# A hybrid decoder layer on one core: the recurrence's copies scheduled ahead on VectorE, softplus summed inside the scan, and small VectorE steps given to ScalarE

## The chip, the cores and the metric

The kernel runs on one core of one Trainium2 chip. The metric is the device time of one execution in microseconds. Three executions of the kernel before took 1123.43, 1123.74 and 1125.81 us; their median, 1123.74 us, is what a change is held against. A further execution was taken by the hardware profiler, and all rows below come from it.

## The reference

One decoder layer on x of 512 tokens by 2048 channels, in float32. `h = rms(x)` is projected by `w_in`; the result is cut into three groups of heads, each computes its own mixing and is multiplied by a SiLU gate, and `w_out` projects all of it back onto the residual.

```python
def step(state, inp):                                   # A: 12 heads of 64, over 512 tokens
    r_t, k_t, v_t, w_t, kk_t, a_t = inp
    sa = einsum('bhvk,bhk->bhv', state, -kk_t)
    state = state * w_t + sa * (kk_t * a_t) + v_t * k_t
    return state, einsum('bhvk,bhk->bhv', state, r_t)
# before it: k = k * (1 + (a - 1) * k_a); after it: a norm per head, a bonus, the gate
d = trailing_mean(u, win) - u;  yb = (d @ pool_w) * pool_scale * silu(pg)          # B
z = rms(q) @ rms(k).T                                   # C: 12 heads, blocks of 128 queries
log_1m = where(causal, log_sigmoid(-z), 0)
after = reverse_cumsum(log_1m) - log_1m
w = where(causal, exp(log_sigmoid(z) + after), 0);  yc = (w @ v) * silu(gc)
x = x + concat([ya, yb, yc]) @ w_out
```

## The kernel before

**Projections.** Everything is laid out with channels on the 128 partitions and the 512 tokens along the free axis. The input projection has 57 column tiles (`tile_order`); three are done at the start from weights that are loaded early (`first`), 54 by `project`. To keep float32 accuracy with fast matmuls, each operand is split in a high and a low part: a weight half (128 x 1024, `raw`) is loaded by DMA, ScalarE casts it to `wh`, VectorE computes `wl = raw - wh`, and each k tile takes three matmuls of 512 columns (`three`: hh with wh, hl with wh, hh with wl). That makes 2592 projection matmuls into `pj` banks and 768 output matmuls into `oacc` banks. `wh` and `wl` have two buffers each. VectorE takes a finished tile out of its bank (`u = pj * rstd`).

**The side tasks.** For each of six pairs of RWKV heads there is a generator `rwkv(p)`, for each of six pairs of attention heads `attention(p)`, and four `pooling(g)`. After every projection matmul `pump()` resumes each task whose next moment has come. `rwkv(p)` first prepares decays and keys, then the mask products `gm`, then inverts 32 x 32 blocks by forward substitution on VectorE (`xblk`, `pr`; the data go through DRAM, `s`), then completes the inverse on TensorE (`q`). Its last part is the recurrence itself, over eight chunks of 64 tokens. Each chunk is a step of three links that depend on each other:

- W: `wus <- uv, amr` on TensorE; VectorE copies it in two halves to `wsb`; GpSimd makes `se`, the decayed state, meanwhile.
- U: `wus <- wsb, lt`; VectorE copies two halves into `uv`.
- S: `wus <- uv, bkt`; VectorE combines it with `se` into the next chunk's `uv`, two instructions. Two y products stand beside.

The page's names for the copies are `wsb<-wus`, `uv<-wus` (COPY, link U) and `uv<-wus,ec,se` (SCALAR_TENSOR_TENSOR, link S). The recurrence of pair p can only begin when that of pair p - 1 is over. `attention(p)` makes z for each head in three blocks (512, 512 and 256 wide), and for each block softplus, a mask, a scan backwards along the keys, a subtraction, a second mask and an exponential; `wT` are the transposed weights.

**What sets the order.** The code is traced in Python, and a scheduler then orders each engine's instructions by priority, which is the order of tracing unless `tc.high_priority(offset=n)` moves an instruction n places ahead. When a task is resumed is decided by the class `Pace`: it keeps a reckoned time `now`, which grows with every matmul, and for each other engine a list of booked stretches. `record` books an instruction in the first free stretch on its engine after its inputs are ready (`place`), and notes when its output will be ready. A task that waits for tiles gives back `need(..., margin)`, and goes on when `now` has passed their reckoned moment plus the margin: MARGIN = 2.5 us, TIGHT = 0.8 us inside the recurrence. The output projection begins when all pairs' tasks are done or forced through; `Y_ORDER` has pair 5 near its end. Scratch tiles come from a ring of TP = 16 buffers.

Of the kernel before, what the change touches and what calls it, by code (L numbers as in the profile page):

```python
# [13 lines left out]
P = 128  # L14
D = 2048
T = 512
# [37 lines left out]
MARGIN = 2.5  # L54
TIGHT = 0.8
AHEAD = 300
EVACUATE = 25
DL = 4.0
TP = 16

# [34 lines left out]
class Pace:  # L95
# [3 lines left out]
    def __init__(self):  # L99
        self.now = 0.0  # L100
        self.ready = {}
        self.read = {}
        self.busy = {"dve": [], "act": [], "pool": []}
        self.slots = {}
        self.queue = 0.0

    @staticmethod
# [103 lines left out]
def hybrid_trunk_kernel(ctx: ExitStack, tc: tile.TileContext, x, xT, w_in, w_out, vecs, consts, up_w, pool_w, out):  # L211
# [58 lines left out]
    bone_r = cp.tile([P, P], F32R, name="bone_r")  # L270
    bmean_r = cp.tile([P, P], F32R, name="bmean_r")
    biases = cp.tile([P, 4], F32, name="biases")
# [3 lines left out]
    nvec = cp.tile([P, 14], F32, name="nvec")  # L276

    def load_constants():
        dma(out=kon, in_=consts)
        dve.tensor_copy(out=bone_r, in_=bone)  # L280
        dve.tensor_scalar(bmean_r, bone, 1.0 / HD, None, ALU.mult)
        dve.tensor_scalar(nvec[:, 0:12], vec[:, V_W0:V_W0 + 12], -1.0, None, ALU.mult)
        dve.tensor_scalar(nvec[:, 12:13], vec[:, V_QN:V_QN + 1], HD ** -0.5, None, ALU.mult)

# [249 lines left out]
    def rwkv(p):  # L534
# [188 lines left out]
        for cc in range(NC_):  # L723
# [5 lines left out]
            wsb = rp.tile([P, C], F32, tag="wsb", bufs=2, name=name("wsb"))  # L729
            dve.tensor_copy(out=wsb[lo, :], in_=wps[lo, 0:C])  # L730
            dve.tensor_copy(out=wsb[hi, :], in_=wps[hi, C:P])
            if not last:
                se = rp.tile([P, C], F32, tag="se", bufs=2, name=name("se"))
                for h, s, o in quad:
                    pool.tensor_scalar(se[s, :], uv[s, cc, h, :], ec[s, cc:cc + 1], None, ALU.mult)
            yield need(wsb, lt, tag="y" if cc % 4 == 0 else None, margin=TIGHT)
# [4 lines left out]
            mm(yps, uv[:, cc, :, :], amr[:, cc, 2:4, :], True, False)  # L741
            dve.tensor_copy(out=uv[lo, cc, 0, :], in_=ups[lo, :])
            dve.tensor_copy(out=uv[hi, cc, 1, :], in_=ups[hi, :])
            yield need(uv, margin=TIGHT + 0.1)
            if not last:
                mm(sps, bkt[:, cc, :], uv[:, cc, :, :])
                for h, s, o in quad:
                    dve.scalar_tensor_tensor(uv[s, cc + 1, h, :], sps[s, h * C:(h + 1) * C], ec[s, cc:cc + 1], se[s, :], ALU.mult, ALU.add)
            mm(yps, uv[:, cc, :, :], rx[:, cc, :, :], False, True)
# [27 lines left out]
    def attention(p):  # L777
# [23 lines left out]
        for h in range(2):  # L801
# [5 lines left out]
            dve.tensor_tensor(q2[other, :], q[s, :], q2[s, :].bitcast(F32), ALU.subtract)  # L807
            dve.tensor_copy(out=k2[s, :], in_=kr[s, :])
            act.copy(out=k2[other, :], in_=k[s, :])
# [4 lines left out]
            for segs, width in ((((3, 0),), 512), (((2, 0), (0, 384)), 512), (((1, 0),), 256)):  # L814
                yield need(q2, k2, kl2, tag="g")
                z = gb("z")
                for i, off in segs:
                    mm(z[:, off:off + (i + 1) * P], q2[:, i * P:(i + 1) * P], k2[:, 0:(i + 1) * P], True, False)
                    mm(z[:, off:off + (i + 1) * P], q2[:, i * P:(i + 1) * P], kl2[:, 0:(i + 1) * P], False, True)
                zz = z[:, 0:width]  # L820
                n = ap.tile([P, 512], F32, tag="n", bufs=2, name=name("n"))
                n = n[:, 0:width]
# [8 lines left out]
                diag = lambda t: t[:, d0:d0 + nd * P].rearrange("p (a t) -> p a t", a=nd) if nd > 1 else t[:, d0:d0 + P]  # L831
                pool.affine_select(out=diag(n), in_=diag(n), pattern=pat, compare_op=ALU.is_gt, fill=0.0, base=0, channel_multiplier=1)
                w = ap.tile([P, width], F32, tag=f"w{segs[0][0]}{h}", name=name("w"))
                for i, off in segs:
# [3 lines left out]
                pool.affine_select(out=diag(w), in_=diag(w), pattern=pat, compare_op=ALU.is_gt, fill=-1e5, base=0, channel_multiplier=1)  # L838
                act.activation(w, w, AF.Exp)
# [16 lines left out]
        for js, width in (((0,), 512), ((1, 3), 512), ((2,), 256)):  # L856
            parts = []
            for h in range(2):
# [259 lines left out]
```

## Time and profile before

| | |
|---|---|
| median of three runs | 1123.74 us |
| the profiled execution | 1124.78 us |
| its span, first to last instruction | 1123.1 us |
| TensorE busy | 1023.5 us, 91% |
| VectorE busy | 733.7 us, 65% |
| ScalarE busy | 427.2 us, 38% |
| GpSimd busy | 228.0 us, 20% |
| mean granted TensorE clock | 0.941 |

Engines stand in the profile as PE (TensorE matmuls), PEld (its weight loads), DVE (VectorE), ACT (ScalarE), POOL (GpSimd) and SP (SyncE, which issues the DMAs). A busy share is an average over the whole span; the stages of this kernel differ, so a window's row tells more. Tile names are those of the program without buffer numbers. Nearly all instructions of VectorE, ScalarE and GpSimd carry one line, that of the helper that records them, so they are found by tile.

### The profile page before, as it was taken

The numbers are of one execution on the slowest core, as the hardware profiler recorded it, in microseconds if no ns is written. First come the engines' busy times: TensorE is split into PE (matmuls) and PEld (weight loads), VectorE is DVE, ScalarE is ACT, GpSimd is POOL, SyncE is SP. The second block draws the span as 40 slices with busy tenths as digits, with TensorE's granted clock in tenths as the row PEclk, the third lists the DMA queues.
The fourth block names the chain that finished last, engine by engine and source line by source line (L and its number), as shares of the span: only waits on it lengthen the run. The fifth ranks groups of instructions, "written<-read, shape, count | busy, mean of one in ns | idle before, by whom it ended". The sixth has DMA issues, their size and how long they took to land.

```text
span 1123.1 us, 13956 instructions
## 1 busy us (share of the span) xinstructions
PE 1023.5 (91%) x5084; PEld 818.0 (73%) x5084; DVE 733.7 (65%) x1554; ACT 427.2 (38%) x658; POOL 228.0 (20%) x330
## 2 busy tenths in 40 slices
PE   8989999899989999999999989999986067999998
PEld 7768777777877778877777777877764055888887
DVE  6278976788779768786797598955774433433232
ACT  6463534543455333652354355423431002312111
POOL 0131310442044112440133114213221010000000
PEclk9999999999999999998999999999995555999999
DMA  8522232131321232212323123232120111833232
GB/s 319 196 79 93 86 103 90 57 98 62 113 80 57 85 104 89 91 70 75 95 84 104 72 75 95 78 115 74 68 103 7 36 33 46 290 133 131 94 131 76
DMA packets 62229, 109.19 MB, mean 97 GB/s; under 512 B 29776, under 2 KB 31184, under 8 KB 62160
## 3 DMA queue, kind: packets, MB, share of 16 engines
q1 hardware_dynamic: 62160, 108.30, 28.7%
q8 instruction: 40, 0.66, 0.2%
q14 instruction: 29, 0.24, 0.1%
HBM read 98.84 MB, written 9.44 MB: 96 GB/s over the span
## 4 chain that ended last, share of the span: by engine, by line
PE 54%; DVE 21%; issue 9%; ACT 6%; POOL 5%; DMA 4%; SPq 0%; DVEq 0%; POOLq 0%; ACTq 0%
PE pj L367 26%; PE oacc L367 16%; DVE wl L205 4%; PE wus L367 4%; POOL e L205 3%; DVE w L205 3%; DVE xblk L205 2%; ACT e L205 2%; DVE pr L205 2%; DVE uv L205 2%; PE first L367 1%; ACT wh L205 1%; PE y L367 1%; DVE u L205 1%; PE o L367 1%
## 5 line engine op out<-in xcount | busy, mean ns | idle before, releaser
L367 PE MATMUL pj<-hh,wl 128*128 128x512 f32 x864 | 346.5, 401 | 6.8 <-DVE wl L205 6.8
L367 PE MATMUL pj<-hh,wh 128*128 128x512 f32 x864 | 346.4, 401 | 0.5 <-DVE u L205 0.4
L367 PE MATMUL pj<-hl,wh 128*128 128x512 f32 x864 | 346.7, 401 | 0.0
L205 DVE TENSOR_TENSOR wl<-raw,wh 128x1024 fp32r<-128x1024 f32 x140 | 175.8, 1256 | 137.6 <-ACT wh L205 137.1
L205 ACT CAST wh<-raw 128x1024 fp32r<-128x1024 f32 x140 | 146.7, 1048 | 296.5 <-PE pj L367 163.8
L367 PEld LDWEIGHTS pj<-hh,wl 128*128 128x128 f32 x864 | 164.2, 190 | 44.1 <-DVE wl L205 11.5
L367 PEld LDWEIGHTS pj<-hh,wh 128*128 128x128 f32 x864 | 164.2, 190 | 36.0 <-issue 4.7
L367 PEld LDWEIGHTS pj<-hl,wh 128*128 128x128 f32 x864 | 164.1, 190 | 34.9 <-issue 2.8
L367 PE MATMUL oacc<-wh,yh 128*128 128x512 f32 x256 | 101.2, 396 | 0.8 <-ACT yh L205 0.8
L367 PE MATMUL oacc<-wl,yh 128*128 128x512 f32 x256 | 101.0, 394 | 0.0
L367 PE MATMUL oacc<-wh,yl 128*128 128x512 f32 x256 | 100.5, 393 | 0.0
L205 POOL TENSOR_SCALAR se<-uv,ec 64x64 f32<-64x64 f32 x84 | 45.4, 541 | 220.8 <-DVE uv L205 202.8
L205 POOL TENSOR_SCALAR e<-e 128x512 f32<-128x512 f32 x28 | 45.4, 1622 | 123.5 <-ACT e L205 101.9
L367 PEld LDWEIGHTS oacc<-wh,yh 128*128 128x128 f32 x256 | 48.9, 191 | 11.6 <-ACT yh L205 1.0
L367 PEld LDWEIGHTS oacc<-wl,yh 128*128 128x128 f32 x256 | 48.8, 191 | 9.9
L367 PEld LDWEIGHTS oacc<-wh,yl 128*128 128x128 f32 x256 | 48.6, 190 | 10.0
L205 POOL TENSOR_TENSOR d<-u 128x512 f32<-128x512 f32 x25 | 36.5, 1461 | 79.0 <-DVE u L205 52.3
L205 DVE TENSOR_TENSOR pr<-xblk,nblk 128x60 f32<-128x60 f32 (+8 forms) x180 | 40.3, 224 | 16.2 <-DMA xblk<-s 9.7
L205 ACT ACTIVATE e<-e 128x512 f32<-128x512 f32 x50 | 31.5, 629 | 40.3 <-POOL e L205 39.8
L205 DVE TENSOR_TENSOR xblk<-xblk,pr 128x60 f32<-128x60 f32 (+8 forms) x180 | 41.4, 230 | 5.3
L205 DVE TENSOR_TENSOR_SCAN w<-kon,n 128x512 f32<-128x512 f32 (+3 forms) x48 | 38.8, 829 | 6.9 <-POOL n L205 6.9
L205 DVE TENSOR_TENSOR u<-pj,rstd 128x512 f32<-128x512 f32 x50 | 34.3, 685 | 11.8 <-PE pj L367 11.3
(204 smaller groups left out, 1353.3 us busy)
## 6 DMA issues: line engine op xcount, KB each, us to landing
raw<-in_w_in SPq DMA_DIRECT2D x108, 512.0 KB, 3.5
raw<-in_w_out SPq DMA_DIRECT2D x32, 512.0 KB, 4.3
lt<-in_x SPq DMA_DIRECT2D x8, 512.0 KB
xr<-in_x SPq DMA_DIRECT2D x16, 256.0 KB, 6.2
out<-xr SPq DMA_DIRECT2D x16, 256.0 KB, 3.6
yin<-yd SPq DMA_DIRECT2D x14, 256.0 KB, 4.0
fr<-in_w_in SPq DMA_DIRECT2D x12, 256.0 KB, 6.2
nblk<-s SPq DMA_DIRECT2D x24, 128.0 KB, 4.1
```

Of the source, the lines that this page charges most:

```text
L205: return call(*args, **kw)
L367: pe.matmul(o, lhsT, rhs, start=start, stop=stop)
```

## The change

`Pace` gets a mark `urgent`. While it is set, an instruction's reckoned end is its inputs' time plus 0.4 us plus its cost, with no booking of the engine. The new context `urgent()` sets it, and raises the priority of what is traced inside by SCAN = 150 places. The wsb copies with the se products, the uv copies, and the state combination of each step stand inside it. TIGHT falls from 0.8 to 0.5, and TP from 16 to 15.

In the attention a block of z is first copied to SBUF by ScalarE and masked there with -1e5; ScalarE makes log(1 + exp(-|w|)) and Relu(w) from the masked copy; the scan adds both operands as it goes, instead of a VectorE addition and a scan against ones; the second mask falls away. The scan over decays is one instruction for eight chunks: its multiplicand `fresh` is 1 except for a 0 at each chunk's first token. To ScalarE go Newton's square and affine step, the k_a step, the copies of transposed values, a cast of k, and one half of the wT copies.

```diff
-TIGHT = 0.8
+TIGHT = 0.5
+SCAN = 150
-TP = 16
+TP = 15
...
-        end = self.place(eng, at, self.cost(eng, f, out, ins))
+        if self.urgent:
+            end = at + 0.4 + self.cost(eng, f, out, ins)
+        else:
+            end = self.place(eng, at, self.cost(eng, f, out, ins))
...
+    @contextmanager
+    def urgent():
+        with tc.high_priority(offset=SCAN):
+            pace.urgent = True
+            yield
+            pace.urgent = False
...
-        dve.tensor_tensor(t, y0, y0, ALU.mult)
+        act.activation(t, y0, AF.Square)
         dve.scalar_tensor_tensor(t, ms, eps, t, ALU.add, ALU.mult)
-        dve.tensor_scalar(t, t, -0.5, 1.5, ALU.mult, ALU.add)
+        act.activation(t, t, AF.Copy, scale=-0.5, bias=1.5)
...
-        for j in range(NC_):
-            cj = slice(j * C, (j + 1) * C)
-            dve.tensor_tensor_scan(c[:, cj], unit.to_broadcast([P, C]), lam[:, cj], 0.0, ALU.mult, ALU.add)
+        dve.tensor_tensor_scan(c, fresh, lam, 0.0, ALU.mult, ALU.add)
...
-        dve.tensor_scalar(a, a, 1.0, col(V_KA), ALU.subtract, ALU.mult)
-        dve.scalar_tensor_tensor(kp, a, 1.0, ks, ALU.add, ALU.mult)
+        act.activation(a, a, AF.Identity, scale=col(V_KA), bias=nvec[:, 13 + p:14 + p])
+        dve.tensor_tensor(kp, a, ks, ALU.mult)
...
-                dve.tensor_copy(out=uv[dst, par::2, h, :], in_=vt4[src, :, h, :])
+                act.copy(out=uv[dst, par::2, h, :], in_=vt4[src, :, h, :])
...
-            dve.tensor_copy(out=wsb[lo, :], in_=wps[lo, 0:C])
-            dve.tensor_copy(out=wsb[hi, :], in_=wps[hi, C:P])
-            if not last:
-                se = rp.tile([P, C], F32, tag="se", bufs=2, name=name("se"))
+            with urgent():
+                dve.tensor_copy(out=wsb[lo, :], in_=wps[lo, 0:C])
+                dve.tensor_copy(out=wsb[hi, :], in_=wps[hi, C:P])
+                if not last:
+                    se = rp.tile([P, C], F32, tag="se", bufs=2, name=name("se"))
...
-                act.activation(n, zz, AF.Abs)
-                act.activation(n, n, AF.Exp, scale=-1.0)
-                act.activation(n, n, AF.Ln, bias=1.0)
-                dve.scalar_tensor_tensor(n, zz, 0.0, n, ALU.max, ALU.add)
...
+                act.copy(out=w, in_=z[:, 0:width])
+                pool.affine_select(out=diag(w), in_=diag(w), pattern=pat, compare_op=ALU.is_gt, fill=-1e5, base=0, channel_multiplier=1)
+                act.activation(n, w, AF.Abs)
+                act.activation(n, n, AF.Exp, scale=-1.0)
+                act.activation(n, n, AF.Ln, bias=1.0)
+                act.activation(m, w, AF.Relu)
...
-                    dve.tensor_tensor_scan(w[:, sg][:, ::-1], unit.to_broadcast([P, (i + 1) * P]), n[:, sg][:, ::-1], 0.0, ALU.mult, ALU.add)
-                dve.tensor_tensor(w, zz, w, ALU.subtract)
+                    dve.tensor_tensor_scan(n[:, sg][:, ::-1], n[:, sg][:, ::-1], m[:, sg][:, ::-1], 0.0, ALU.add, ALU.add)
+                dve.tensor_tensor(w, w, n, ALU.subtract)
...
-                (dve.tensor_copy if h == 0 else act.copy)(out=wt, in_=tps[:, 0:width])
+                act.copy(out=wt, in_=tps[:, 0:width])
```

TensorE's order in the first step of pair 5's recurrence. Before, it stands behind the last projection matmul, and its links follow each other directly (wus are the links, y the products beside them):

```order
L367 MATMUL wus_7782<-uv_7769,amr_95 128x128
L367 MATMUL y_7791<-amr_95,uv_7769 128x128
L367 MATMUL wus_7782<-wsb_7784,lt_97 128x64
L367 MATMUL wus_7782<-uv_7769,bkt_7755 128x128
L367 MATMUL y_7791<-rx_7295,uv_7769 128x128
L367 MATMUL wus_7799<-uv_7769,amr_95 128x128
```

With the change, the same step stands in the projection (pj), after 2414 of its 2592 matmuls:

```order
L377 MATMUL wus_7483<-uv_7427,amr_98 128x128
L377 MATMUL pj_7445<-hh_105,wl_7376 128x512
L377 MATMUL pj_7445<-hh_106,wh_7375 128x512
L377 MATMUL pj_7445<-hl_122,wh_7375 128x512
L377 MATMUL pj_7445<-hh_106,wl_7376 128x512
L377 MATMUL pj_7445<-hh_107,wh_7375 128x512
L377 MATMUL pj_7445<-hl_123,wh_7375 128x512
L377 MATMUL pj_7445<-hh_107,wl_7376 128x512
L377 MATMUL wus_7483<-wsb_7485,lt_100 128x64
L377 MATMUL y_7499<-amr_98,uv_7427 128x128
```

Seven projection matmuls stand between links W and U, where none did.

VectorE's order in the first step of the second recurrence, pair 1. Before, from the wsb copies to the uv copies of the U link (lt, amr and rx are pair 2's mask products):

```order
L205 COPY wsb_3408<-wus_3406 64x64 x2
L205 TENSOR_TENSOR lt_96<-gm_3422,kon 64x4x64
L205 TENSOR_TENSOR amr_94<-gm_3422,kon 64x4x64
L205 TENSOR_TENSOR rx_3304<-gm_3422,kon 128x4x64
L205 TENSOR_TENSOR lt_96<-gm_3423,kon 64x4x64
L205 TENSOR_TENSOR amr_94<-gm_3423,kon 64x4x64
L205 TENSOR_TENSOR rx_3304<-gm_3423,kon 128x4x64
L205 COPY uv_3291<-wus_3406 64x64 x2
```

With the change, the same step and the beginning of the next:

```order
L210 COPY wsb_2837<-wus_2835 64x64 x2
L210 TENSOR_TENSOR cq_2664<-u_2654,qs_2665 128x512
L210 TENSOR_TENSOR sl_2827<-qs_2824,sh_2826 128x512
L210 COPY uv_2746<-wus_2835 64x64 x2
L210 TENSOR_SCALAR sq_2753<-ss_2869 128x512
L210 TENSOR_TENSOR q_505_3079<-cq_2664,q_505_3079 64x512
L210 SCALAR_TENSOR_TENSOR uv_2746<-wus_2835,ec_1764,se_2840 64x64 x2
L210 SCALAR_TENSOR_TENSOR c_2875<-fresh,e_2846 128x512
L210 COPY wsb_2898<-wus_2896 64x64 x2
```

The copies of successive links now have one or two wide instructions between them (the row c<-fresh is the single scan).

## Rows read from the trace of the kernel before

**Rows 1.** The page: busy time by engine, and the granted clock in 40 slices.
```profile
PE 1023.5 (91%) x5084; PEld 818.0 (73%) x5084; DVE 733.7 (65%) x1554; ACT 427.2 (38%) x658; POOL 228.0 (20%) x330
...
PEclk9999999999999999998999999999995555999999
```

**Rows 2.** Windows: stretch, length, busy us of each engine (count), clock, DMA.
```profile
60.00:841.00 781.00, 745.09 (x3884) 595.07 (x3882) 603.09 (x1278) 344.53 (x543) 210.94 (x289) 0.98 0.26 86
...
841.40:949.00 107.60, 52.79 (x221) 37.39 (x222) 43.32 (x160) 9.77 (x19) 8.82 (x22) 0.51 0.08 20
...
112.00:140.00 28.00, 26.39 (x119) 21.30 (x118) 26.71 (x60) 15.94 (x29) 10.81 (x16) 1.00 0.26 87
...
833.00:843.00 10.00, 8.96 (x48) 6.41 (x47) 6.34 (x21) 1.35 (x3) 2.93 (x6) 1.00 0.00 1
...
949.00:1119.50 170.50, 170.34 (x745) 140.55 (x743) 55.72 (x61) 38.87 (x43) 0.00 (x0) 0.99 0.42 145
```

**Rows 3.** Timeline of TensorE, 829 to 900 us: start, length, instruction, [idle before <- what ended it].
```profile
829.63 0.80 PE L367 MATMUL oacc<-wh,yh 128*128 128x512 f32 x1 [0.82 <-ACT yh L205]
...
845.00 0.79 PE L367 MATMUL wus<-uv,amr 128*128 128x128 f32 x2 [0.27 <-DVE uv L205]
...
849.25 0.76 PE L367 MATMUL wus<-uv,amr 128*128 128x128 f32 x2 [0.36 <-DVE uv L205]
...
899.98 0.28 PE L367 MATMUL q<-xt,lt 32*32 32x32 f32 x2 [32.66 <-DVE xt L205]
```

**Rows 4.** Timeline of TensorE, 838 to 842 us, recurrence steps among output matmuls.
```profile
838.16 0.38 PE L367 MATMUL wus<-uv,amr 128*128 128x128 f32 x2
...
838.52 0.47 PE L367 MATMUL oacc<-wh,yl 128*128 128x512 f32 x1
838.83 0.40 PE L367 MATMUL oacc<-wh,yh 128*128 128x512 f32 x1
839.09 0.43 PE L367 MATMUL wus<-wsb,lt 128*128 128x64 f32 x2
839.34 0.48 PE L367 MATMUL oacc<-wl,yh 128*128 128x512 f32 x1
...
841.43 0.46 PE L367 MATMUL wus<-uv,amr 128*128 128x128 f32 x2 [0.56 <-DVE uv L205]
```

**Rows 5.** Who waited for tile wus, 60 to 841 us; timeline around 800 us.
```profile
  PE wus L367: 13.7, 10
...
799.82 0.75 DVE L205 SCALAR_TENSOR_TENSOR u<-po,vec,u 128x512 f32<-128x512 f32 x1 [2.34 <-POOL u L205]
...
801.00 0.43 PE L367 MATMUL wus<-wsb,lt 128*128 128x64 f32 x2 [2.27 <-DVE wsb L205]
```

**Rows 6.** VectorE's groups by form: count, busy us, mean ns, idle before.
```profile
L205 DVE TENSOR_TENSOR wl<-raw,wh 128x1024 fp32r<-128x1024 f32 x140 | 175.8, 1256 | 137.6 <-ACT wh L205 137.1
...
L205 DVE SCALAR_TENSOR_TENSOR n<-z,n 128x512 f32<-128x512 f32 x24 | 16.1, 680 | 6.9 <-ACT n L205 6.8
L205 DVE TENSOR_TENSOR_SCAN w<-kon,n 128x512 f32<-128x512 f32 x12 | 14.8, 1237 | 4.5 <-POOL n L205 4.5
...
L205 DVE TENSOR_TENSOR_SCAN c<-kon,e 128x64 f32<-128x64 f32 x48 | 10.5, 280 | 14.8 <-ACT e L205 14.7
...
L205 DVE COPY uv<-vt 64x256 f32<-64x256 f32 x24 | 10.1, 422 | 3.4 <-PE vt L371 3.0
...
L205 DVE TENSOR_TENSOR qs<-y 128x512 f32<-128x512 f32 x12 | 9.3, 772 | 3.5 <-ACT y L205 3.4
```

**Rows 7.** ScalarE's groups by form.
```profile
L205 ACT ACTIVATE n<-n 128x512 f32<-128x512 f32 x48 | 29.0, 627 | 0.5
...
L205 ACT COPY yc<-y 64x256 f32<-64x256 f32 x24 | 8.7, 364 | 61.8 <-PE y L367 61.6
```

**Rows 8.** Timeline of GpSimd around 500 us and 916 us: pairs of se.
```profile
500.18 2.64 POOL L205 TENSOR_SCALAR se<-uv,ec 64x64 f32<-64x64 f32 x2
...
916.33 0.97 POOL L205 TENSOR_SCALAR se<-uv,ec 64x64 f32<-64x64 f32 x2 [3.26 <-DVE uv L205]
```

More of the change, by code (lines that the diff above doesn't have):

```diff
@@ L1 @@
 import math
-from contextlib import ExitStack
+from contextlib import ExitStack, contextmanager
 import concourse.bass as bass
@@ L105, in __init__ @@
         self.queue = 0.0
+        self.urgent = False
     @staticmethod
@@ L271, in hybrid_trunk_kernel @@
     bmean_r = cp.tile([P, P], F32R, name="bmean_r")
+    fresh = cp.tile([P, T], F32, name="fresh")
+    pool.memset(fresh, 1.0)
+    pool.memset(fresh[:, 0:T:C], 0.0)
     biases = cp.tile([P, 4], F32, name="biases")
@@ L275, in hybrid_trunk_kernel @@
     eps_rms, eps_gn, neg_half = biases[:, 0:1], biases[:, 1:2], biases[:, 2:3]
-    nvec = cp.tile([P, 14], F32, name="nvec")
+    nvec = cp.tile([P, 20], F32, name="nvec")
     def load_constants():
@@ L282, in load_constants @@
         dve.tensor_scalar(nvec[:, 0:12], vec[:, V_W0:V_W0 + 12], -1.0, None, ALU.mult)
+        dve.tensor_scalar(nvec[:, 13:19], vec[:, V_KA:V_KA + 6], -1.0, 1.0, ALU.mult, ALU.add)
         dve.tensor_scalar(nvec[:, 12:13], vec[:, V_QN:V_QN + 1], HD ** -0.5, None, ALU.mult)
@@ L729, in rwkv @@
             wsb = rp.tile([P, C], F32, tag="wsb", bufs=2, name=name("wsb"))
-            dve.tensor_copy(out=wsb[lo, :], in_=wps[lo, 0:C])
-            dve.tensor_copy(out=wsb[hi, :], in_=wps[hi, C:P])
-            if not last:
-                se = rp.tile([P, C], F32, tag="se", bufs=2, name=name("se"))
-                for h, s, o in quad:
-                    pool.tensor_scalar(se[s, :], uv[s, cc, h, :], ec[s, cc:cc + 1], None, ALU.mult)
+            with urgent():
[3 more added lines that the diff above has]
+                    se = rp.tile([P, C], F32, tag="se", bufs=2, name=name("se"))
+                    for h, s, o in quad:
+                        pool.tensor_scalar(se[s, :], uv[s, cc, h, :], ec[s, cc:cc + 1], None, ALU.mult)
             yield need(wsb, lt, tag="y" if cc % 4 == 0 else None, margin=TIGHT)
@@ L741, in rwkv @@
             mm(yps, uv[:, cc, :, :], amr[:, cc, 2:4, :], True, False)
-            dve.tensor_copy(out=uv[lo, cc, 0, :], in_=ups[lo, :])
-            dve.tensor_copy(out=uv[hi, cc, 1, :], in_=ups[hi, :])
+            with urgent():
+                dve.tensor_copy(out=uv[lo, cc, 0, :], in_=ups[lo, :])
+                dve.tensor_copy(out=uv[hi, cc, 1, :], in_=ups[hi, :])
             yield need(uv, margin=TIGHT + 0.1)
@@ L746, in rwkv @@
                 mm(sps, bkt[:, cc, :], uv[:, cc, :, :])
-                for h, s, o in quad:
-                    dve.scalar_tensor_tensor(uv[s, cc + 1, h, :], sps[s, h * C:(h + 1) * C], ec[s, cc:cc + 1], se[s, :], ALU.mult, ALU.add)
+                with urgent():
+                    for h, s, o in quad:
+                        dve.scalar_tensor_tensor(uv[s, cc + 1, h, :], sps[s, h * C:(h + 1) * C], ec[s, cc:cc + 1], se[s, :], ALU.mult, ALU.add)
             mm(yps, uv[:, cc, :, :], rx[:, cc, :, :], False, True)
@@ L807, in attention @@
             dve.tensor_tensor(q2[other, :], q[s, :], q2[s, :].bitcast(F32), ALU.subtract)
-            dve.tensor_copy(out=k2[s, :], in_=kr[s, :])
+            act.copy(out=k2[s, :], in_=k[s, :])
             act.copy(out=k2[other, :], in_=k[s, :])
@@ L819, in attention @@
                     mm(z[:, off:off + (i + 1) * P], q2[:, i * P:(i + 1) * P], kl2[:, 0:(i + 1) * P], False, True)
-                zz = z[:, 0:width]
-                n = ap.tile([P, 512], F32, tag="n", bufs=2, name=name("n"))
-                n = n[:, 0:width]
-                act.activation(n, zz, AF.Abs)
-                act.activation(n, n, AF.Exp, scale=-1.0)
-                act.activation(n, n, AF.Ln, bias=1.0)
-                dve.scalar_tensor_tensor(n, zz, 0.0, n, ALU.max, ALU.add)
                 d0 = segs[0][0] * P
@@ L831, in attention @@
                 diag = lambda t: t[:, d0:d0 + nd * P].rearrange("p (a t) -> p a t", a=nd) if nd > 1 else t[:, d0:d0 + P]
-                pool.affine_select(out=diag(n), in_=diag(n), pattern=pat, compare_op=ALU.is_gt, fill=0.0, base=0, channel_multiplier=1)
                 w = ap.tile([P, width], F32, tag=f"w{segs[0][0]}{h}", name=name("w"))
+                act.copy(out=w, in_=z[:, 0:width])
+                pool.affine_select(out=diag(w), in_=diag(w), pattern=pat, compare_op=ALU.is_gt, fill=-1e5, base=0, channel_multiplier=1)
+                n = ap.tile([P, 512], F32, tag="n", bufs=2, name=name("n"))[:, 0:width]
+                m = ap.tile([P, 512], F32, tag="m", bufs=1, name=name("m"))[:, 0:width]
+                act.activation(n, w, AF.Abs)
+                act.activation(n, n, AF.Exp, scale=-1.0)
+                act.activation(n, n, AF.Ln, bias=1.0)
+                act.activation(m, w, AF.Relu)
                 for i, off in segs:
                     sg = slice(off, off + (i + 1) * P)
-                    dve.tensor_tensor_scan(w[:, sg][:, ::-1], unit.to_broadcast([P, (i + 1) * P]), n[:, sg][:, ::-1], 0.0, ALU.mult, ALU.add)
-                dve.tensor_tensor(w, zz, w, ALU.subtract)
-                pool.affine_select(out=diag(w), in_=diag(w), pattern=pat, compare_op=ALU.is_gt, fill=-1e5, base=0, channel_multiplier=1)
+                    dve.tensor_tensor_scan(n[:, sg][:, ::-1], n[:, sg][:, ::-1], m[:, sg][:, ::-1], 0.0, ALU.add, ALU.add)
+                dve.tensor_tensor(w, w, n, ALU.subtract)
                 act.activation(w, w, AF.Exp)
```

## The prediction

> **What bounds the kernel now.** I read the page's totals first. TensorE is busy 1023.5 of 1123.1 us, and the row of granted clock shows a full clock almost everywhere except for a hole near the end [rows 1]. The table of windows sizes that hole [rows 2]. From 60 to 841 us TensorE is busy 745.1 of 781 us at clock 0.98; from 841.4 to 949 us it is busy only 52.8 of 107.6 us, at 0.51; from 949 us on it is busy without a gap (745 matmuls in 170.3 us, so 0.2286 us each). The reader is to see three stages: a nearly full one, a hole of 107.6 us, a full one.
>
> The timeline of TensorE says what the hole is [rows 3]. With the last projection matmuls done, the recurrence of pair 4 still has four steps to go, and the whole of pair 5's follows: half of its mask products, 32.66 us of waiting for the block inverse that runs through VectorE and DMA, then eight steps. A step alone, at half clock, takes 4.25 us from one W matmul to the next (845.00 to 849.25), and TensorE waits within it for VectorE's copies. So the bound here is a dependent chain with nothing left to put between. The output projection doesn't fill it: two of its first four accumulators take g banks, which the recurrence still uses, and TensorE's order has them behind it.
>
> Why are the recurrences so late? In the first stage a step's matmuls don't stand close together: the order spreads the eight steps of one recurrence over 409 to 518 projection matmuls. The pace reckons each copy behind all the work booked on VectorE, and emits the next link only when that reckoning lets it. The chain itself is faster: where only a few output matmuls stood between, at full clock, W to W took 3.27 us (838.16 to 841.43) [rows 4].
>
> **The change, the reckoning.** With the copies marked urgent and TIGHT at 0.5, the order has each recurrence inside 129 to 164 wide matmuls (6 or 7 between two links), and the sixth is over at projection matmul 2558 of 2592, before the output projection begins. The hole's cause is gone: **minus 107.6 us**. Its matmuls have to be issued all the same, between others and at full clock: 52.8 us busy at a granted 0.51 is **plus 26.9 us** at full clock. A check from the other side [rows 4]: W with its y product takes 0.36 us to the next wide matmul (838.16 to 838.52), S with its own about as much, U 0.25, and each return to a wide matmul costs 0.08 (0.47 against 0.40), some 1.2 us a step; the 12 steps of the hole are 14.5 us, and the mask products, norms, transposes and block products an estimated 8 more. I take 26.9 and keep 22 as its lower bound.
>
> **What the copies cost now.** Behind a link stand only 6 or 7 matmuls of 0.2286 us, so with its own matmuls about 1.8 us from link to link, where the chain alone needs about 1.1 (3.27 / 3) [rows 4]. What VectorE does between two copies therefore decides. Summed by shape at the trace's mean durations, the instructions between the first and the last copy of the second recurrence (92 of them, five wl splits of 1.256 us among them [rows 6]) take 43.8 us; TensorE's work in the same stretch, 130 wide matmuls, eight steps and some small products, takes 42.8. The other recurrences read alike (51.4 against 51.7, 43.1 against 42.5, 44.4 against 43.0, 43.8 against 42.5), and only the last has room (26.6 against 42.9). The two engines are level, and tied to each other three times a step. The most that VectorE reaches in a long stretch of before is 26.71 of 28 us, 0.95 [rows 2]: 226.5 us of its work over five recurrences at 0.95 is 238, against 222.5 on TensorE, so **plus 16 us** of stalls. Lower bound: its records overlap (they sum to 6% over its busy time), and 213 at 0.95 is 224, plus 2. Upper bound: adding, link by link, what VectorE's work exceeds TensorE's, with nothing made up between, gives plus 34.
>
> On the other side stand the stalls of the old order: in the first stage TensorE waited 13.7 us for wsb and uv copies, ten times [rows 5]. One is shown: VectorE stood 2.34 us at a pooling instruction that waited for GpSimd, then worked 0.75 us on it, and U came 2.27 us late [rows 5]. These go with the old places of the copies: **minus 13.7 us**. In-order waits of this kind can return at the new places; that is in the upper bound.
>
> The output projection now begins with no hole ahead in which its first tiles are loaded. Its first matmul waited 0.82 us for yh [rows 3]; four k tiles split in a hurry would be **plus 3 us**, bounds 0 and 5.
>
> **The change, the engines.** VectorE loses the softplus add (16.1 us for the wide form), the copies of transposed values (10.1), Newton's square (9.3) and smaller steps; the 48 short scans (10.5 us) become 6 of 1.24 us, 7.4 [rows 6]. In all some 60 to 70 of its 734 us, already out of the sums above. A scan of two tiles isn't in the trace; the nearest row scans one tile against a broadcast, 1.237 us [rows 6]. I take that; a fifth more on each of the wide ones would be about 3 us, inside the upper bound. ScalarE gets some 80 us: at 0.627 a wide activation, 0.364 a quarter copy [rows 7], two more instructions per softplus block (copy out, Relu) and the moved copies. It was busy 344.5 of 781 us in the first stage [rows 2], so it goes to about 54%. What hides it is the time in which it sits waiting for TensorE to release wh. Without that cover a late wh makes wl late and the next half tile waits; I price that at nothing, bound 8 us, ten waits of 0.8. GpSimd loses one select a block, off the path. In the attention, ScalarE's first activation now waits for a select behind its own copy, and what is queued behind it, wh among it, waits too; it does so 36 times on an engine that is idle 45% of the time. The scratch ring loses one buffer of 16, which no wait that I read is put down to: nothing. SP's queue keeps its transfers in their relation to the recurrences.
>
> A rule bears on GpSimd's se products, which each step's S copies need. The trace has a pair of them at 0.97 us in the hole, but 2.64 us at 500 us, beside VectorE's wl [rows 8]. The Trainium skill, SBUF — State Buffer, section Who interferes with whom, states that a VectorE instruction with two SBUF inputs and a GpSimd instruction that reads SBUF lock each other out; by that rule, the trace agrees. The packed recurrences put such VectorE work beside every se, and the change makes the w subtraction one more of that kind. The pair has over 5 us, from one S copy to the next, so I price it at nothing.
>
> **The sum.** Against the profiled execution's span: 1123.1 - 107.6 + 26.9 + 16 - 13.7 + 3 = 1047.7, a change of -75.4. That execution took 1124.8, the median of the runs is 1123.7, so **1048 us**.
>
> **The rivals.**
> Level engines cost nothing: the copies come before TensorE asks, and the lighter VectorE delivers wl in time too. 1123.7 - 107.6 + 22 + 2 - 13.7 - 2 = 1024. For it: the last recurrence has this room. Against it: in-order waits as at 800 us.
>
> Part of the hole stays: one block inverse is late, and TensorE stands for it in the middle of the projection as long as in the hole, 32.66 us [rows 3]. 1048 + 33 = 1081. Against it: 196 to 267 projection matmuls stand between a pair's mask products and its block product, 45 us and more.
>
> The clock falls in the packed recurrences. At 843 us it fell to half, right behind waits of 0.56 us and less [rows 2, 4], and a matmul then takes twice as long. A quarter of 222 us at half clock is plus 55: 1103. Against it: from 833 to 843 us, with a few output matmuls between the links, it was granted 1.00 [rows 2]. The Trainium skill, TensorE: Matmul & The Clock Gate, section A second HAM failure mode, describes short idles between groups of matmuls that make the clock swing, which would be this case.
>
> GpSimd's se comes late at every step: 40 steps by 1.67 us (2.64 - 0.97) is plus 67, 1115. By the rule above this is the price when nothing hides it.
>
> Slower than before: the marks place the copies early by reckoning, but VectorE runs in order, and an instruction that waits for another engine holds up the copies behind it as at 801 us. If each of the 48 steps meets one such stall of 2.27 us [rows 5], that is plus 109: 1123.7 - 107.6 + 26.9 + 109 = 1152. It decides once a step stalls over 1.7 us ((107.6 - 26.9) / 48). Against it: in VectorE's new order mostly one to four instructions stand between the copies of one link and the next, and few of them wait for GpSimd.
>
> **How the numbers follow.** Forecast 0.56; nothing lost 0.20; part of the hole 0.08; clock 0.07; se late 0.05; slower 0.04. A measurement of this kernel can tell 0.2%, some 2 us. Faster by more than that 0.95, within it 0.01, slower 0.04. The range leaves out clock, se and slower, 0.16 in all: from 1020 (nothing lost, and 4 us of wl waits gone) to 1085 (the forecast with 34 in place of 16, 8 for ScalarE and 5 for the start is 1076; part of the hole 1081).
>
> **What would show it.** Right: no stretch at clock 0.5 between the last projection matmul and the output projection, whose start is near 875 us and whose length stays 170; waits for wsb and uv of 10 to 40 us; VectorE's busy time near 665, ScalarE's near 505. Wrong: 5s in the clock row inside the first stage, single waits over 5 us for xt, or VectorE over 90% busy with TensorE below 80% in a recurrence.

## The result, and the profile after

The changed kernel takes 1056.84 us (median of four runs, 1054.38 to 1057.74), the kernel before 1123.97 beside it: a ratio of 0.9397, 95% interval 0.9377 to 0.9416. The forecast was 1048 us in a range of 1020 to 1085. The profiled execution has a span of 1054.6 us, 68.5 less than before; the forecast had 75.4 less.

The page of the changed kernel, totals and granted clock, answers to [rows 1]:

```profile
PE 997.9 (95%) x5084; PEld 792.9 (75%) x5084; DVE 683.0 (65%) x1393; ACT 497.5 (47%) x814; POOL 219.8 (21%) x296
...
PEclk9999999999999999999999999999999998999999
```

The four 5s are gone. What is left of them is one 8, and its place is the start of the output projection. The windows (stretch, length, busy us of each engine with its count, granted clock, DMA) answer to [rows 2]; the last projection matmul is over at 864.0 us:

```profile
60.00:864.00 804.00, 763.33 (x4081) 600.57 (x4079) 590.15 (x1269) 418.65 (x709) 208.76 (x273) 1.00 0.26 83
864.00:880.00 16.00, 7.66 (x23) 5.43 (x22) 9.41 (x14) 11.65 (x19) 2.76 (x2) 0.68 0.71 246
880.00:1051.00 171.00, 170.61 (x752) 140.77 (x750) 53.29 (x56) 34.51 (x35) 0.00 (x0) 1.00 0.39 136
```

**Where the 68.5 us went.** The first stage of before, up to its hole, lasted 781.4 us. I reckon 6.3 of them for the 24 output matmuls that stood in it (24 x 0.2286, and the wait of 0.82); 775.1 are comparable. The first stage of after lasts 804.0, and has all six recurrences in it: +28.9. The hole is gone: -107.6. From the end of the first stage to the last matmul the changed kernel takes 187.0 us (864.0 to 1051.0); before it was 170.5 and the same 6.3, so +10.2. Sum: -107.6 + 28.9 + 10.2 = -68.5. The forecast had +29.2 (26.9 + 16 - 13.7) for the second number, and +3 for the third. So its error of 6.9 us is that of the third number, 7.2, less 0.3.

That start, in the timelines of TensorE, ScalarE, SP's queue and VectorE (start, length, instruction, [idle before <- what ended it]):

```profile
872.20 0.79 PE L377 MATMUL oacc<-wh,yh 128*128 128x512 f32 x1 [8.16 <-ACT yh L210]
...
877.18 0.45 PE L377 MATMUL oacc<-wl,yh 128*128 128x512 f32 x1
877.46 0.39 PE L377 MATMUL oacc<-wh,yl 128*128 128x512 f32 x1
```

```profile
865.33 0.60 ACT L210 CAST yh<-y 128x512 fp32r<-128x512 f32 x1
865.84 0.61 ACT L210 CAST sh<-sq 128x512 fp32r<-128x512 f32 x1
868.04 0.63 ACT L210 ACTIVATE e<-u 128x512 f32<-128x512 f32 x1 [1.60 <-DVE u L210]
870.35 1.29 ACT L210 ACTIVATE e<-e 128x512 f32<-128x512 f32 x2 [1.68 <-POOL e L210]
871.55 1.97 ACT L210 CAST yh<-yin 128x512 fp32r<-128x512 f32 x3
```

```profile
853.27 13.24 SPq L224 DMA_DIRECT2D raw<-in_w_out  x3
866.60 1.81 SPq L224 DMA_DIRECT2D yin<-yd  x4
```

TensorE stands 8.16 us for a cast. In ScalarE's order that cast stands behind the sigmoid of the last pooling gate, which waits 1.60 us for VectorE and 1.68 us for GpSimd. The gate itself is late: VectorE takes its tile (u) out of the bank only at 867.27, 3.6 us after the start of the last projection matmul (863.65), because wl and two more splits stand ahead of it in VectorE's order. The input yin of the cast stands on SP's queue behind a weight load that waits for its buffer, and was issued only at 866.60. TensorE stood from 864.0 us on; from 867.0 to 877.2 us its granted clock was 0.50 (1.2 GHz, the lower of its two levels), and the first output matmuls are 0.43 us apart until then.

```profile
864.92 1.23 DVE L210 TENSOR_TENSOR wl<-raw,wh 128x1024 fp32r<-128x1024 f32 x1 [0.85 <-ACT wh L210]
...
867.27 0.68 DVE L210 TENSOR_TENSOR u<-pj,rstd 128x512 f32<-128x512 f32 x1
```

### The profile page after: what moved, and what is told of

The parts are those of the page before. It is cut to its first block, busy times and chain, and to the rows that moved or that the text cites. A ratio compares the mean times of both kernels' runs of the same rounds, so it can differ in the third digit from the quotient of the medians.

```text
span 1054.6 us, 13939 instructions
## 1 busy us (share of the span) xinstructions
PE 997.9 (95%) x5084; PEld 792.9 (75%) x5084; DVE 683.0 (65%) x1393; ACT 497.5 (47%) x814; POOL 219.8 (21%) x296
## 4 chain that ended last, share of the span: by engine, by line
PE 47%; DVE 23%; issue 13%; ACT 7%; POOL 6%; DMA 3%; SPq 0%; POOLq 0%; DVEq 0%; ACTq 0%
PE pj L377 22%; PE oacc L377 17%; DVE wl L210 4%; POOL e L210 3%; DVE pr L210 2%; DVE xblk L210 2%; DVE n L210 2%; DVE uv L210 2%; PE first L377 2%; ACT e L210 2%; DVE u L210 1%; DMA lt<-in_x 1%; DVE amr L210 1%; ACT n L210 1%; ACT wh L210 1%
## 5 line engine op out<-in xcount | busy, mean ns | idle before, releaser
L210 POOL TENSOR_SCALAR se<-uv,ec 64x64 f32<-64x64 f32 x84 | 55.5, 660 | 92.8 <-DVE uv L210 87.9
L210 DVE TENSOR_TENSOR_SCAN n<-n,m 128x512 f32<-128x512 f32 (+3 forms) x48 | 40.5, 861 | 18.2 <-ACT n L210 15.8
L210 DVE TENSOR_TENSOR pr<-xblk,nblk 128x60 f32<-128x60 f32 (+8 forms) x180 | 44.4, 247 | 4.9
L210 DVE TENSOR_TENSOR xblk<-xblk,pr 128x60 f32<-128x60 f32 (+8 forms) x180 | 43.6, 242 | 5.0
```

Source lines behind the costliest of these rows:

```text
L210: return call(*args, **kw)
```

## The experiments

All times are medians of device time, beside the kernel before on the same chip (1124.0 to 1125.1 us).

**The order without the engine moves, and the engine moves without the order.**

```diff
 e1: kernel before, and:
-TIGHT = 0.8
+TIGHT = 0.5
+SCAN = 150
...
+            with urgent():
                 dve.tensor_copy(out=wsb[lo, :], in_=wps[lo, 0:C])
 e2: changed kernel, and:
-TIGHT = 0.5
+TIGHT = 0.8
-        with tc.high_priority(offset=SCAN):
-            pace.urgent = True
+        if True:
+            pace.urgent = False
```

> The kernel before, with the order of the change alone: the urgent reckoning, the raised priority and TIGHT 0.5, but no step moved off VectorE. The last recurrence now overlaps the end of the projection and the first 170 output matmuls. Theory (the order brings the gain, the lighter VectorE only keeps the links supplied): the hole of 107.6 us is gone, its matmuls cost 26.9 us, and VectorE, 60 to 70 us heavier over the whole first stage, is some 20 us heavier inside the recurrences, which comes on top of the 16 us of stalls: about 1068 us, 1060 to 1085. Rival (the lighter engines are what pays): over 1095 us.

> The changed kernel without its order: no urgent reckoning, no raised priority, TIGHT 0.8, but all moves between the engines. The recurrences are again spread over 290 to 400 projection matmuls each, and all of pair 5's stands behind the last projection matmul. Theory (the order brings the gain): eight steps of 4.25 us and part of the 32.66 us for the block inverse stay as a hole at half clock, 50 to 75 us; against the changed kernel 35 to 50 us slower, 1090 to 1108 us. Rival (the lighter engines bring it): within 10 us of the changed kernel's 1057.

Measured: the order alone 1080.1 us (ratio 0.9597, 0.9576 to 0.9617), the engine moves alone 1079.6 (0.9599, 0.9570 to 0.9628). Each by itself brings 45 of the 67 us, so they overlap. The order alone came out inside the theory's range, 12 us above its 1068. The engine moves alone came out 10 us below the theory's range and 13 above the rival's: they shrink the hole too. The table of windows of that kernel, around its remaining hole:

```profile
60.00:840.00 780.00, 742.50 (x3964) 593.12 (x3962) 563.45 (x1204) 411.22 (x690) 208.56 (x255) 0.99 0.28 86
840.00:900.00 60.00, 40.91 (x144) 29.43 (x142) 25.82 (x73) 15.01 (x29) 10.13 (x20) 0.66 0.10 35
```

`place` books the links in VectorE's free stretches, and a lighter VectorE has them earlier. In this kernel two steps of pair 4 stand behind the last projection matmul, where in the kernel before seven did, and pair 5's eight steps follow without the long wait for the block inverse. The prediction counted the engine moves as room for the copies alone, and not as something that moves the planned order. No single move was run by itself, nor was TP, which is 16 in the first of these kernels and 15 in the second.

**Which part of the order.** All four kernels have the engines of the change and TIGHT 0.5; they differ in the mark `pace.urgent` and in `tc.high_priority`.

```diff
 e3: changed kernel, and:
-        with tc.high_priority(offset=SCAN):
+        if True:
 e4: changed kernel, and:
-            pace.urgent = True
+            pace.urgent = False
 e10: changed kernel, and both
```

> The changed kernel with the urgent reckoning but without the raised priority. TensorE's order is nearly the same as in the changed kernel (the six recurrences begin at the same projection matmuls); VectorE's copies stand where they are traced. If the reckoning alone makes the gain: 1055 to 1065 us. If the priority is needed, because VectorE meets the copies behind work that was traced ahead of them, each of 140 links loses half a wide instruction, 0.3 us and more: 1095 us or above.

> The changed kernel with the raised priority but the old reckoning of VectorE. The recurrences keep 277 to 352 projection matmuls each, pair 4's ends at 2523 of 2592, and pair 5's falls into the last 40 projection matmuls and behind them. Theory (position decides): most of the eight steps of pair 5 stand alone at 4.25 us, a hole of 25 to 40 us, less some stalls that the wider spacing saves: 1070 to 1090 us. If priority were what matters: 1057 us.

> The changed kernel with TIGHT 0.5 but neither the urgent reckoning nor the raised priority; TensorE's recurrences stand at the same projection matmuls as with the priority alone (1052.6 us). If the priority is worth as much here as it was under the reckoning (1069.4 against 1056.8, 12.6 us): 1062 to 1068 us. If the recurrences, spread over 277 to 352 projection matmuls, don't need it, and TIGHT alone made the 27 us between 1079.6 and 1052.6: 1051 to 1055 us.

| TIGHT 0.5 | no raised priority | raised priority |
|---|---|---|
| old reckoning | 1068.5 | 1052.6 |
| urgent reckoning | 1069.4 | 1056.8 (the change) |

The raised priority is worth 12.6 us with the urgent reckoning and 15.9 without it. The urgent reckoning is worth nothing (0.9 and 4.2 us slower; the intervals of the second pair, 0.9377 to 0.9416 and 0.9338 to 0.9380, just overlap). From 1079.6 to 1068.5 leads TIGHT alone. Three of my expectations missed. The reckoning alone, 1069.4 us, lies between its two branches; the kernel with neither, 1068.5, just above the branch in which the priority counts. The priority alone lies 17 us below the theory's range, and the theory behind it, that the place of the recurrences decides, falls. The windows of that kernel (priority alone) show the trade:

```profile
60.00:841.50 781.50, 752.12 (x4006) 600.57 (x4006) 576.55 (x1223) 417.68 (x702) 204.47 (x263) 0.98 0.28 86
841.50:880.00 38.50, 28.02 (x108) 19.87 (x107) 21.61 (x56) 12.19 (x22) 8.31 (x13) 0.73 0.21 64
880.00:1048.00 168.00, 167.25 (x738) 138.14 (x736) 55.05 (x60) 36.80 (x40) 0.00 (x0) 1.00 0.44 147
```

A rest of the hole stays, 38.5 us at clock 0.73 with 10.5 us idle. But the first stage, which lacks most of pair 5's steps and has the other five recurrences spread over 325 to 352 projection matmuls each (115 to 150 in the changed kernel), is idle for 29.4 us where the changed kernel's is idle for 40.7. TensorE waits for the links' copies for 16.4 us in it, against 27.0, and its first output matmul waits 0.44 us for yh, against 8.16. Removing the hole by packing is paid back in stalls of the packed links and in a late start of the output projection.

**What the stalls at the links are made of.** In the changed kernel TensorE waited 27.0 us for wsb and uv in the first stage, 34 times, where [rows 5] had 13.7 in ten. The view of tile wus, and that of TensorE's waits from 60 to 864 us (who waited <- for what: us in total, times, longest):

```profile
  PE wus L377: 27.0, 34
```

```profile
PE wus L377 <- DVE uv L210: 15.8, 23, 1.9
PE wus L377 <- DVE wsb L210: 11.1, 11, 2.7
PE pj L377 <- DVE wl L210: 6.7, 6, 2.2
```

The longest of them, read in the timelines of VectorE and TensorE:

```profile
355.55 1.27 DVE L210 TENSOR_TENSOR_SCAN n<-n,m 128x384 f32<-128x384 f32 x2 [1.89 <-ACT n L210]
356.93 0.69 DVE L210 TENSOR_TENSOR w<-w,n 128x512 f32<-128x512 f32 x1
357.54 1.22 DVE L210 TENSOR_TENSOR wl<-raw,wh 128x1024 fp32r<-128x1024 f32 x1
358.79 0.46 DVE L210 COPY wsb<-wus 64x64 f32<-64x64 f32 x2
```

```profile
359.30 0.43 PE L377 MATMUL wus<-wsb,lt 128*128 128x64 f32 x2 [2.73 <-DVE wsb L210]
```

VectorE stands 1.89 us at a scan whose input ScalarE makes late (the scan's two operands, n and m, are now four activations behind a copy and a select), then does 3.1 us of work, and the copies stand behind it all. Link by link, 15.8 us in ten waits of over 0.4 us follow such an in-order wait of VectorE, eight of them at a scan; eleven more, 7.8 us, follow work with no such wait in it, or with one under 0.9 us. Four kernels bear on what that costs.

More room for each link:

```diff
-TIGHT = 0.5
+TIGHT = 1.2
```

> The changed kernel with TIGHT 1.2 in place of 0.5: the recurrences stand over 175 to 195 projection matmuls instead of 118 to 150, some 8 to 9 between two links. Theory (the stalls are VectorE's queue between the links, level with TensorE): TensorE's 27.0 us of waits for wsb and uv fall to 8 to 15, and the time to 1040 to 1048 us. Rival (the stalls come from single in-order waits on VectorE, wherever the links stand): waits of 22 to 30 us, and 1055 to 1060 us.

Measured 1051.3 us, 5.6 faster and between the two expectations, but the waits for wsb and uv, at 29.7 us instead of 27.0, are the rival's. The gain has another place. Pair 5's last step now stands behind the last projection matmul, in the time in which TensorE waits for yh; the first output matmul waited only 1.57 us for it and began at 866.08 us, 6.1 earlier than in the changed kernel. Room between the links does not take the stalls away.

More and less work for VectorE:

```diff
 e8: changed kernel, and between links U and S of each step
+            nc.vector.tensor_copy(out=fresh, in_=fresh)
 e9: changed kernel, without scan and subtraction
-                for i, off in segs:
-                    sg = slice(off, off + (i + 1) * P)
-                    dve.tensor_tensor_scan(n[:, sg][:, ::-1], n[:, sg][:, ::-1], m[:, sg][:, ::-1], 0.0, ALU.add, ALU.add)
-                dve.tensor_tensor(w, w, n, ALU.subtract)
-                act.activation(w, w, AF.Exp)
+                act.activation(w, n, AF.Exp)
```

> The changed kernel with one more VectorE instruction in each of the 48 steps, a copy of 128 x 512 that nothing else needs, between links U and S; the reckoning does not know of it, so that TensorE's order stays. It adds some 0.6 us a step by the other wide instructions, 29 us in all. Theory (VectorE is level with TensorE inside the recurrences): 20 to 29 us come through, 1077 to 1086 us. Rival (VectorE has room there): under 8 us, up to 1065.

> The changed kernel with the scan and the subtraction of the attention left out (the exponential takes the softplus itself, so the attention is not computed): some 70 us less VectorE work over the first stage, about 20 of it inside the recurrences. The reckoning knows of it, and the recurrences begin 50 to 140 projection matmuls earlier, as densely as before. Theory (level engines): the 27.0 us of waits for wsb and uv fall to 5 to 12, and the time to 1035 to 1045 us. Rival (the stalls are the chain's own response time, with whatever load): waits over 20 us, and 1052 to 1058.

The added copy is shorter than I had taken (VectorE's groups by form: count, busy us, mean ns, idle before):

```profile
L762 DVE COPY fresh<-fresh 128x512 f32<-128x512 f32 x48 | 22.9, 477 | 0.9
```

VectorE was busy 19.1 us longer, and the time was 1064.0 us (ratio 0.9461, 0.9443 to 0.9479), 7.1 more. By the time the rival holds (under 8 us, up to 1065), but the work was less than either branch had taken, and 0.37 of it came through: VectorE is neither level nor free. With the work left out (the attention is then not computed) VectorE was busy 61.8 us less, and the time was 1030.9 us (0.9170, 0.9152 to 0.9189), 25.9 less: 0.42 of it. That is 4 us below the theory's range, though the waits for wsb and uv, 12.9 us, stayed just above the 5 to 12 that it had. TensorE's waits of that kernel, 60 to 864 us:

```profile
PE wus L377 <- DVE uv L210: 9.7, 14, 1.9
...
PE wus L377 <- DVE wsb L210: 3.2, 4, 1.8
PE pj L377 <- DVE wl L210: 2.7, 4, 1.5
```

So one us of VectorE is worth about 0.4 us in this kernel, over a range from 19 more to 62 less. The first comparison gives a like number: from the order alone to the change VectorE's busy time falls by 52.1 us (735.1 to 683.0), and the time by 23.3, or 0.45. But there pair 5's recurrence moves too, from behind the last projection matmul into the projection, so that number is no third measurement of the same thing. "Level engines" was half right: more than half of such work still finds idle time.

The in-order waits themselves taken away:

```diff
+SLACK = 0.0
+        yield need(lam, margin=SLACK)
         dve.tensor_tensor_scan(c, fresh, lam, 0.0, ALU.mult, ALU.add)
...
+                yield need(n, m, margin=SLACK)
                 for i, off in segs:
```

> The changed kernel, with the scans of the attention and of the decays handed to VectorE only when the reckoning has their inputs from ScalarE ready: one more place where the task is put off, no instruction more or less. Theory (over half of the stalls at the links, 15.8 of 28.4 us, are VectorE standing in its order at a scan that waits for ScalarE, with the copies behind it): the waits of this kind fall under 6 us and the time to 1047 to 1052 us. Rival (VectorE's work itself is what the copies wait for): the waits change their name only, 1054 to 1060 us.

Measured 1055.9 us (0.9389, 0.9365 to 0.9414), no different from the change. The waits did what the theory said: those behind an in-order wait of VectorE fell from 15.8 to 4.8 us. But the time did not follow, and the view of TensorE's waits shows where it went:

```profile
PE wus L378 <- DVE uv L211: 15.1, 21, 1.9
PE pj L378 <- DVE wl L211: 11.9, 11, 1.4
PE pj L378 <- ACT wh L211: 4.0, 6, 1.9
PE wT L382 <- ACT w L211: 2.7, 1, 2.7
PE wus L378 <- DVE wsb L211: 1.4, 5, 0.6
```

The waits for wsb went from 11.1 to 1.4 us, those for wl and wh from 6.9 to 15.9. The sum of TensorE's idle time in the first stage went from 40.7 to 38.7, and its busy time from 763.3 to 769.2, so that the stage was 4 us longer in the execution that was profiled, the slowest of the four. The stalls change their name: taking away this wait alone gives nothing. That it is the amount of VectorE's work that decides agrees with the two kernels above, and is not shown beyond them; why the waits return at wl was not tried.

**The start of the output projection.** First the loads alone, on another queue:

```diff
-                dma(out=yin[i], in_=yd[n])
+                dma(out=yin[i], in_=yd[n], queue=nc.gpsimd)
```

> The changed kernel with one edit: the loads of the mixed tiles for the output projection (yin) are issued by GpSimd's queue, not by SP's, where they stand behind a weight load that waits 13.24 us for its buffer. Theory (that queue makes the first output matmul 8.16 us late, and the late start makes the 10.2 us at half clock): 8 to 13 us faster, 1044 to 1049 us, no idle time over 2 us at the first output matmul. Rival (the last pooling gate on ScalarE and GpSimd is late by itself): 1055 to 1058 us, with the same wait for yh.

Measured 1057.0 us, with 8.19 us of waiting for yh: my first theory, SP's queue, falls, and the rival holds. The first tile's load was issued at 846.14 us on GpSimd's queue, and its cast still ran at 869.83, behind the gate's activations. Then the loads and the casts together:

```diff
-                yin[i] = tmp("yin")
-                dma(out=yin[i], in_=yd[n])
+                if i < 5:
+                    tag, bufs = (("n", 2), ("n", 2), ("m", 1), ("w30", 1), ("w31", 1))[i]
+                    yin[i] = ap.tile([P, T], F32, tag=tag, bufs=bufs, name=name("yin"))
+                else:
+                    yin[i] = tmp("yin")
+                with tc.high_priority(offset=400 if i < 5 else 0):
+                    dma(out=yin[i], in_=yd[n])
...
-        act.copy(out=yh[k], in_=yin[i])
-        dve.tensor_tensor(yl[k], yin[i], yh[k].bitcast(F32), ALU.subtract)
+        with tc.high_priority(offset=400 if i < 4 else 0):
+            act.copy(out=yh[k], in_=yin[i])
+            dve.tensor_tensor(yl[k], yin[i], yh[k].bitcast(F32), ALU.subtract)
```

> The changed kernel, with the first five tiles of the output projection brought in early: their loads go to buffers that the attention has left and are raised ahead of the weight loads, and their casts and subtractions stand ahead of the last pooling gate on ScalarE and VectorE. Theory (the output projection begins 10 us late because the cast yh stands on ScalarE behind the gate's two activations, which wait for VectorE and GpSimd, and its load behind weight loads): the idle time of 8.16 us and most of the half clock behind it go, and the time is 1045 to 1049 us. Rival (the casts, now among the last steps of the recurrence, take from its links what they give): 1054 us or more.

Measured 1045.3 us (0.9291, 0.9273 to 0.9309), 11.5 us faster than the change. ScalarE now casts five tiles inside the last projection tile, and TensorE goes from the last projection matmul to the first output matmul without a gap and at full clock (timelines of ScalarE and TensorE, then windows):

```profile
851.77 3.35 ACT L210 CAST yh<-yin 128x512 fp32r<-128x512 f32 x5 [0.31 <-PE pj L377]
```

```profile
863.56 0.40 PE L377 MATMUL pj<-hh,wl 128*128 128x512 f32 x1
863.80 0.40 PE L377 MATMUL oacc<-wh,yh 128*128 128x512 f32 x1
864.03 0.39 PE L377 MATMUL oacc<-wl,yh 128*128 128x512 f32 x1
```

```profile
60.00:863.80 803.80, 764.18 (x4079) 601.60 (x4077) 592.15 (x1273) 421.49 (x714) 208.56 (x273) 0.99 0.27 85
863.80:1040.00 176.20, 175.83 (x773) 144.63 (x771) 58.53 (x65) 42.73 (x49) 2.78 (x2) 1.00 0.43 147
```

The first stage is as long as before the edit (803.8 against 804.0), the rest 10.8 us shorter (176.2 against 187.0): the whole loss of 10.2 us was this start.

**All together.** The early start, the scans put off and TIGHT 1.2:

> Three edits together: the early start of the output projection, the scans put off, and TIGHT 1.2. Theory: their gains come from different waits, so they add to what TIGHT 1.2 alone gave (1051.3 us): 4 to 5 us at the start of the output projection and 5 to 9 us of in-order waits, 1037 to 1043 us. Rival (with TIGHT 1.2 only 9.7 us of stalls are in-order waits, and the start is already early): 1046 to 1051 us.

Measured 1044.3 us (0.9283, 0.9265 to 0.9301), between the two expectations, and not to be told from the early start alone. That fits what the other two gave by themselves: the scans put off gave nothing, and the gain of TIGHT 1.2 lay at the start that is now early. Both are faster than the kernel before and the change.

## Why the prediction was right, and where a term was off

- **The hole** (-107.6 and its matmuls at full clock, +26.9): right. The hole is gone, and TensorE's busy time in the first stage rose by 23.7 us (763.3 against 745.1 less 24 output matmuls of 0.2286), between the lower bound of 22 and the value taken. The first stage's granted clock rose from 0.98 to 1.00 as well, which the forecast had no term for; what that gave is in the 23.7 and was not separated. One reading was wrong and changed no term: behind the last projection matmul pair 4 had seven steps to go, not four. Four were left at 841.4 us, where the sum begins.
- **The stalls** (+16 for level engines, bounds 2 and 34, and -13.7 for those of the old order): the waits for wsb and uv are 27.0 us, not 16, inside the 10 to 40 that the prediction named. The difference was made good by what it didn't reckon: TensorE's other idle time in the first stage fell from 21.8 to 13.7 us (35.5 less 13.7, and 40.7 less 27.0). The sum came out right, 28.9 against 29.2, by luck: 11.0 more of stalls met 8.1 of other idle time and 3.2 of matmul time that it had not taken off. The reason given, VectorE level with TensorE, is shown at 0.4 us for one us, not at 1.
- **The start of the output projection** (+3, bounds 0 and 5): the mis-sized term; it measured 10.2. The step that failed: its price was taken from the wait of 0.82 us in [rows 3], a first output matmul with gaps all about it, and the tiles were counted (four splits) instead of what stands ahead of them in ScalarE's order. There the sigmoid of the last gate stands, three activations with an instruction of GpSimd between them and 3.28 us of waiting, and it can't begin before the last projection matmul is over. The 0.82 us were only the end of this wait. In the kernel before the same gate stood between the start of the last projection matmul (823.83) and the first output matmul (829.63), but VectorE took its tile 0.4 us after the former and not 3.6, and links of pair 4 filled part of the time. In TensorE's rows these 5.8 us have 3.54 of idle time, 2.72 of them put down to the copies of the links (timelines of VectorE, ScalarE and TensorE):

```profile
824.25 0.69 DVE L205 TENSOR_TENSOR u<-pj,rstd 128x512 f32<-128x512 f32 x1 [1.92 <-PE pj L367]
```

```profile
827.77 1.29 ACT L205 ACTIVATE e<-e 128x512 f32<-128x512 f32 x2 [1.34 <-POOL e L205]
828.97 1.65 ACT L205 CAST yh<-yin 128x512 fp32r<-128x512 f32 x3
```

```profile
826.70 0.49 PE L367 MATMUL wus<-uv,bkt 128*128 128x128 f32 x2 [2.04 <-DVE uv L205]
...
828.09 0.49 PE L367 MATMUL wus<-uv,amr 128*128 128x128 f32 x2 [0.68 <-DVE uv L205]
```

- **The signs named**: the output projection began at 872.2 us, near the 875 named. It lasted 178.4 us and not 170, which was the time of the 745 matmuls behind the hole, where 768 stand now. And a stretch at clock 0.50 did stand ahead of it, from 867.0 us, in the wait for yh.
- **The engines**: VectorE 683.0 us, not 665 (it lost 50.7 us, not 60 to 70); ScalarE 497.5, not 505. ScalarE's load cost nothing at wl, as priced: TensorE waited 6.7 us for it, and 6.8 before. The softplus scan with two operands took 1283 ns, against the row of 1237 ns that was taken for it [rows 6].

```profile
L210 DVE TENSOR_TENSOR_SCAN n<-n,m 128x512 f32<-128x512 f32 x12 | 15.4, 1283 | 8.0 <-ACT n L210 7.8
```

- **The rivals**: level engines did not cost nothing, as the 27.0 us of waits show. No wait for xt stands in TensorE's first stage, so no part of the hole stayed. The clock stayed at 1.00 through the packed recurrences, so that one fell. No copy of link S waits for GpSimd's se in the trace, so se late fell as well, though its pairs got longer (below). The slower case had the right mechanism, VectorE held in its order by an instruction that waits for another engine, but ten times and not at each of 48 steps.
- **What the forecast credited to the wrong cause**: it put the gain down to the urgent reckoning, and the engine moves only as room. The reckoning can be left out; the priority, TIGHT and the lighter VectorE bring the gain, and overlap.

## What to carry to other kernels

When a change moves work away from the seam between two stages, list what that work covered: every instruction that the next stage's first step needs, and what stands ahead of each in its engine's order and queue. Price work on a shared in-order engine by adding and taking away some: here one us of VectorE was worth 0.4 us over 80 us of change, and one kind of wait, when it was removed, came back under another name. A planner's tables react to the load as well as to their own constants, so an edit that only moves work between engines also moves the order.

## What the runs showed of the hardware that was not expected

A pair of se on GpSimd, 64 x 64 each, took 5.42 us in the changed kernel, where a free pair takes 0.97 [rows 8] (timeline of GpSimd, and of VectorE beside it):

```profile
82.75 5.42 POOL L210 TENSOR_SCALAR se<-uv,ec 64x64 f32<-64x64 f32 x2
```

```profile
84.33 0.67 DVE L210 TENSOR_TENSOR sl<-qs,sh 128x512 fp32r<-128x512 f32 x1
84.93 0.67 DVE L210 TENSOR_TENSOR e<-e,d 128x512 f32<-128x512 f32 x1
85.53 0.67 DVE L210 TENSOR_TENSOR cq<-u,qs 128x512 f32<-128x512 f32 x1
86.13 1.21 DVE L210 TENSOR_TENSOR wl<-raw,wh 128x1024 fp32r<-128x1024 f32 x1
```

From 84.33 us on VectorE ran instructions with two SBUF inputs back to back, and one of the two se, begun at 84.12, lasted 4.06 us. The Trainium skill, SBUF — State Buffer, section Who interferes with whom, states that a VectorE instruction with two SBUF inputs contends with a GpSimd instruction that reads SBUF. The trace agrees: that se, at 4.06 us, lasted over several such instructions, where the median of the 84 is 0.44. That the contention is the cause was not tried by itself. Of the 84 se 13 took over 1 us, against 4 before; no instruction of VectorE is shown waiting for one.
